# Sums over the keys by GpSimd in place of products with ones, in a decoder layer on one Trainium2 core

## The chip, the core and the metric

The kernel runs on one core of a Trainium2 chip. The core has a matrix engine (TensorE, PE in the profile, with PEld for its weight loads), a vector engine (VectorE, DVE), an engine for activation functions (ScalarE, ACT), a general engine (GpSimd, POOL) and an engine that only issues DMA transfers (SyncE, SP). Each works through its own queue in order and waits on semaphores for the others. TensorE writes to PSUM, a small memory of banks; the other engines read from there. The metric is the device time of one execution in microseconds, as the median of several runs.

## The reference

One decoder layer with a sequence of 512 tokens and a width of 1024, in float32. Two attentions run side by side on one projection of the normed input, and are merged behind gates:

```python
u = rms_norm(x, norm_mix_g[i])
proj = u @ w_in[i]
q_sb, k_sb, v_sb, q_dl, k_dl, v_dl, gate_sb, gate_dl = jnp.split(proj, SPLITS, axis=-1)
o_sb = stick_breaking_attention(heads_sb(q_sb), heads_sb(k_sb), heads_sb(v_sb))
o_dl = dilated_mixture_attention(heads_dl(q_dl), heads_dl(k_dl), heads_dl(v_dl)).astype(x.dtype)
merged = jax.nn.sigmoid(gate_sb) * (o_sb @ w_sb_up[i]) + jax.nn.sigmoid(gate_dl) * (o_dl @ w_dil_up[i])
x = x + merged @ w_out[i]
u2 = rms_norm(x, norm_ffn_g[i])
g_ff, up_ff = jnp.split(u2 @ w_ffn_in[i], 2, axis=-1)
x = x + (jax.nn.silu(g_ff) * up_ff) @ w_ffn_out[i]
```

Both attentions need a sum over keys. Stick-breaking (8 heads of 64) weighs key k for a query by exp(log sigmoid(z) + the sum of log sigmoid(-z) over the keys after k and before the query):

```python
log_keep = jnp.where(causal, jax.nn.log_sigmoid(-z), 0.0)
log_after = lax.cumsum(log_keep, axis=3, reverse=True) - log_keep
a = jnp.where(causal, jnp.exp(jax.nn.log_sigmoid(z) + log_after), 0.0)
```

The dilated attention (three groups of 4 heads, with window and dilation of their own and a bias by distance) is a softmax over the keys of all three groups; its denominator is a sum of exponentials over keys:

```python
p = jnp.exp(scores - m[..., None])
l = p.sum(-1)
...
den = (wts * jnp.stack(ls)).sum(0)
out = num / den[..., None]
```

## The kernel before

Activations lie with features on the 128 partitions and the 512 tokens in the free dimension. A weight chunk is 128 x 1024 numbers. Each number is split in two, a rounded high part and a low part (`hi`, `lo`), and `mm3` makes each product of three matmuls (lines 158 to 160): high by high, low by high, high by low. `weights(i, ahead=2)` keeps the split of chunks two ahead of the products: SyncE issues the load (line 111), ScalarE rounds (`whi`, line 143), VectorE takes the difference (`wlo`, line 144). `product` calls `tick()` after every three matmuls. The attentions are Python generators that are resumed at these ticks, so that their matmuls are issued between those of the projections; a `yield n` waits n ticks, and `can_take` waits until one of three pairs of PSUM banks is free (`take`, `give`). A planner that simulates the engines' time then fixes each engine's queue, by priorities and readiness. For the instructions on TensorE in the feed-forward part the order is written by hand.

*The beginning.* The first two weight chunks and the eight slices of x (tiles `x`, two slices each) are loaded in parts, one beside the other, on SyncE's queue; the norms' weights (`gt`, 128x24) by GpSimd's DMA queue (line 173). `norm_split` (lines 177 and 178) multiplies a slice of x by the norm's weight and splits it into `xh` and `xl`. The row factors of the norm are applied later, to the products. The first two products (`first`, query and key of pair 0) begin as the parts land. Behind the last split of x (`last_split`) ScalarE squares the four tiles of x (line 226), which VectorE adds up to `acc1`; the row sums over it (line 264) come on TensorE some ticks into the product for the values (`pvvs`), the first that uses the third weight chunk.

*Stick-breaking.* `sb_pair` handles two heads, four times. Scores are made with keys on the partitions in three parts: x holds query blocks 1 to 3 against key block 1 and query block 3 against key block 3 (128 x 2 x 512 in all), y key block 2 (128 x 2 x 256), z key block 0. `breaks` makes t = softplus of the scores from three activations and line 431, and splits it (lines 163 and 164). `weigh` adds the sums over later keys within the block by a product with a triangle of minus ones (line 439), and takes the exponential. What lies between blocks is a factor exp(-sum of t over all keys of a later block): `side` (line 446) multiplies t with ones on TensorE, so that each of the 64 partitions of a head holds the sum, the tile `b` takes these sums (parts x and y), and line 476 makes their exponentials `f` in one instruction on 128x768. `side` with values makes the weighted values, in `b` (part y) and `a`, and lines 486 to 492 put the blocks together with `f`.

*Dilated.* `dil_pair` handles two heads of each group, twice. Four score tiles `p` get the bias (line 519). The maximum over the groups is taken on VectorE, and over the partitions by GpSimd, `partition_all_reduce` (line 528), which leaves the result in every partition. After exponentials (lines 532 to 537) the groups are added to `mb` (lines 538 to 540). The numerator is `pn` (line 550). The denominator `dl` is a product of `mb` with ones (line 555), in a bank pair of its own; line 558 takes its reciprocal.

After the projections of the gates come the up-projections (`up`, whose second part reads the dilated output `ohd`), the output projection (`po`), and the feed-forward part with weights in seven forms (`pf`, `pg`) and the way down (`pd`). The residual is loaded by GpSimd's DMA queue (line 645).

Of the kernel before, what the change touches and what calls it, by code (L numbers as in the profile page):

```python
# [10 lines left out]
F32 = mybir.dt.float32  # L11
# [32 lines left out]
def trunk_kernel(ctx, tc, xT, gains, w_in, w_up, w_o, w_f, w_d, bias, out):  # L44
# [20 lines left out]
    def bank(tag, name):  # L65
# [4 lines left out]
        return pair(name)[:, 0, :]  # L70


    warm = cp.tile([P, P], BF16)
# [42 lines left out]
    def split_chunk(i):  # L116
# [24 lines left out]
        if kind in ("S23", "S1"):  # L141
            hi, lo = (t.rearrange("p (a n) -> p a n", a=2) for t in (hi, lo))
        A.copy(hi, r)  # L143
        V.tensor_tensor(out=lo, in0=r, in1=hi.bitcast(F32), op=ALU.subtract)  # L144
# [25 lines left out]
    fpool = [None]  # L170
    gt = cp.tile([P, 24], F32)
    g32 = cp.tile([P, KD], F32)
    nc.gpsimd.dma_start(out=gt, in_=gains)

# [38 lines left out]
    for k in range(KD):  # L213
# [4 lines left out]
        lo = xp.tile([P, S], F32R, tag=f"xl{k}", name=f"xl{k}")  # L218
        last_split = norm_split(k, xw[k // 2][:, k % 2, :], 0, hi, lo)
        if k % 2 == 0:  # L220
            split_to(parts[1][0][:, cs], parts[1][1][:, cs], raws[1][:, cs])
        xh.append(hi)
        xl.append(lo)
    with tc.high_priority():
        for x in xw:
            i = A.activation(x, x, AF.Square)
            tc.add_manual_dep(i.ins, last_split.ins.name, NOSYNC, reason="issue order")
        V.tensor_tensor(out=xw[0], in0=xw[0], in1=xw[1], op=ALU.add)
        V.tensor_tensor(out=xw[2], in0=xw[2], in1=xw[3], op=ALU.add)
        V.tensor_tensor(out=xw[0], in0=xw[0], in1=xw[2], op=ALU.add)  # L230
        V.tensor_tensor(out=acc1, in0=xw[0][:, 0, :], in1=xw[0][:, 1, :], op=ALU.add)
# [180 lines left out]
    def sb_pair(n, q, k, v, hb, done):  # L412
# [11 lines left out]
        def breaks(name, ps, w):  # L424
# [7 lines left out]
            split_to(hi, lo, t)  # L432
            return ps, t, hi, lo, lambda: new(f"e{n}{name}")


        def weigh(ps, t, hi, lo, new):
            for m in (hi, lo):
# [6 lines left out]
        def side(o, lhs, rhs, first):  # L444
            for h in range(2):
                T.matmul(o[hs[h]], lhs(h), rhs[:, h, :], start=first, stop=False, skip_group_check=True)

        yield can_take
        bx = breaks("x", scores("x", [(1, 0), (3, 384)]), S)
# [17 lines left out]
        val = lambda a: lambda h: v()[:, a, (hb + h) * 64:(hb + h + 1) * 64]  # L467
        one = lambda h: ones[:, :64]
        yield lambda: v() is not None
        yield can_take  # L470
        pb = take(f"b{n}")
        side(pb[:, 1, 0:384], one, bx[1][:, :, 0:384], True)
        side(pb[:, 1, 384:512], one, bx[1][:, :, 384:512], False)
        side(pb[:, 0, 256:512], one, by[1], True)
        f = wide(f"f{n}").rearrange("p a b -> p (a b)")[:, 256:1024]
        A.activation(f, pb.rearrange("p a b -> p (a b)")[:, 256:1024], AF.Exp, scale=-1.0)
        side(pb[:, 0, 0:256], val(2), ey, False)
        done.append(n)
# [28 lines left out]
    def dil_pair(n, q, k, v):  # L507
# [31 lines left out]
        V.tensor_tensor(out=by_block(mb), in0=by_block(t0), in1=by_token(m), op=ALU.add)  # L539
        V.tensor_tensor(out=mb[:, :, P:], in0=mb[:, :, P:], in1=t3[:, :, P:], op=ALU.add)  # L540
        yield 36
        yield lambda: v() is not None
        yield can_take
        pn = take(f"n{n}")
        for g in (1, 2, 0, 3):
            o = pn[:, int(g in (1, 2)), :]
            for c in range(g // 3, 4):
                for h in range(2):
                    cl = (2 * n + h) * 64
                    T.matmul(o[hs[h], cb[c]], v()[g % 3][:, c - g // 3, cl:cl + 64], tl[g][hs_all, h, cb[c]],  # L550
                             start=g < 2 and c == 0, stop=g > 1 and c == 3, skip_group_check=True)
        yield can_take
        pl = take(f"dl{n}")[:, 0, :]
        for h in range(2):
            T.matmul(pl[hs[h]], ones[:, :64], mb[:, h, :], start=True, stop=True)
        rl, nb = small(f"rl{n}"), small(f"nb{n}")
        A.copy(nb, pn[:, 1, :])
        V.reciprocal(rl, pl)
        nt = small(f"nt{n}")
        one = lambda t: t.unsqueeze(1)  # L560
        V.tensor_tensor(out=by_block(one(nt)), in0=by_block(one(pn[:, 0, :])), in1=by_token(one(nb)), op=ALU.add)
        V.tensor_tensor(out=rl, in0=nt, in1=rl, op=ALU.mult)
        give(6)
        give(6)
# [435 lines left out]
```

## Time and profile before

| | |
|---|---|
| median of the runs | 766.88 us (765.97, 766.88, 768.06) |
| the profiled execution's own time | 768.07 us |
| its span | 766.4 us |
| mean granted clock of TensorE | 0.995 |

The profile is of one execution. A row of a view in order of time gives start and duration in us, engine, line, operation, output <- input, shapes, and a count where neighbours are merged; the bracket says how long the engine had been idle and what ended it. A row of a tile's view gives minimum, median and maximum duration in ns, first and last start in us, and the forms. A row of stretches gives the length and for each engine its busy time with the number of instructions; its last row the sums. Matmuls overlap, and their ends are modelled: the distance between starts tells what one costs. Spans on POOL are rough.

### The profile page before, as it was taken

Reading aid. Unit: us, or ns where it says so; the run is one execution under the profiler, and the core shown is the slowest. Engines: PE = TensorE matmul, PEld = TensorE weight load, DVE = VectorE, ACT = ScalarE, POOL = GpSimd, SP = SyncE. Lnnn points to the kernel's source line nnn. Section 1 sums busy time; section 2 is a strip of 40 time slices with the busy share of each in tenths; the row PEclk is TensorE's granted clock in tenths of the full one; section 3 lists DMA queues with packets and bytes.
Section 4 is the critical chain, followed back from the end, with each engine's and each line's share of the span. In section 5 each row is a group of like instructions: output and inputs, shape, how many; then the busy total and the mean of one; then the engine's idle time right before and its main releaser. Section 6 shows DMA issues by size and latency. Waiting matters only on the chain. (4 is left out here: it accounts for less than half of the span.)

```text
span 766.4 us, 11025 instructions
## 1 busy us (share of the span) xinstructions
PE 753.4 (98%) x4498; PEld 646.6 (84%) x4498; DVE 511.6 (67%) x685; ACT 358.6 (47%) x509; POOL 29.0 (4%) x38
## 2 busy tenths in 40 slices
PE   8999999999999999999999999999999999999996
PEld 5877767798887878888788999999999999999985
DVE  6454646344677775358698989877788777776643
ACT  7273727462233352333455666544445454444453
POOL 1000000000101100000000100000000000000032
PEclk9999999999999999999999999999999999999998
DMA  7312121123224223233432223323333323332113
GB/s 247 137 56 83 56 83 56 56 69 124 83 83 159 88 84 103 62 91 129 145 103 79 75 89 103 103 79 122 98 106 114 103 82 113 100 105 77 56 55 111
DMA packets 24947, 74.13 MB, mean 97 GB/s; under 512 B 2736, under 2 KB 5824, under 8 KB 24768
## 3 DMA queue, kind: packets, MB, share of 16 engines
q1 hardware_dynamic: 23664, 69.87, 28.3%
q0 software_dynamic: 816, 3.16, 1.3%
q8 instruction: 35, 0.57, 0.3%
q10 hardware_dynamic: 416, 0.39, 0.2%
q14 instruction: 16, 0.13, 0.1%
HBM read 71.32 MB, written 2.10 MB: 96 GB/s over the span
## 5 line engine op out<-in xcount | busy, mean ns | idle before, releaser
L143 ACT CAST whi<-raw 128x1024 fp32r<-128x1024 f32 (+2 forms) x113 | 108.5, 962 | 160.8 <-issue 49.2
L144 DVE TENSOR_TENSOR wlo<-raw,whi 128x1024 fp32r<-128x1024 f32 (+2 forms) x113 | 125.9, 1115 | 34.4 <-ACT whi L143 33.6
L756 PE MATMUL pf<-fh,whi 128*128 128x256 f32 x348 | 98.8, 284 | 0.4 <-ACT q L763 0.3
L758 PE MATMUL pf<-fh,wlo 128*128 128x256 f32 x348 | 98.5, 283 | 0.0
L757 PE MATMUL pf<-fl,whi 128*128 128x256 f32 x348 | 98.5, 283 | 0.0
L756 PE MATMUL pg<-fh,whi 128*128 128x256 f32 x264 | 75.1, 285 | 0.6 <-ACT q L763 0.6
L757 PE MATMUL pg<-fl,whi 128*128 128x256 f32 x264 | 74.7, 283 | 0.0
L758 PE MATMUL pg<-fh,wlo 128*128 128x256 f32 x264 | 74.7, 283 | 0.0
L756 PEld LDWEIGHTS pf<-fh,whi 128*128 128x128 f32 x348 | 66.7, 192 | 1.5 <-ACT q L763 0.8
L757 PEld LDWEIGHTS pf<-fl,whi 128*128 128x128 f32 x348 | 66.7, 192 | 0.6
L758 PEld LDWEIGHTS pf<-fh,wlo 128*128 128x128 f32 x348 | 66.7, 192 | 0.3 <-DVE wlo L144 0.2
L144 DVE TENSOR_TENSOR wlo<-s,whi 128x1024 fp32r<-128x1024 f32 (+1 forms) x43 | 41.3, 960 | 15.9 <-ACT whi L143 15.7
L756 PEld LDWEIGHTS pg<-fh,whi 128*128 128x128 f32 x264 | 50.6, 192 | 1.1 <-ACT q L763 0.8
L143 ACT CAST whi<-s 128x1024 fp32r<-128x1024 f32 (+1 forms) x43 | 36.2, 841 | 32.6 <-PE pg L757 20.5
L757 PEld LDWEIGHTS pg<-fl,whi 128*128 128x128 f32 x264 | 50.7, 192 | 0.0
L758 PEld LDWEIGHTS pg<-fh,wlo 128*128 128x128 f32 x264 | 50.6, 192 | 0.0
L158 PE MATMUL pd<-hh,whi 128*128 128x512 f32 (+1 forms) x132 | 50.4, 382 | 0.0
L159 PE MATMUL pd<-hl,whi 128*128 128x512 f32 (+1 forms) x132 | 50.3, 381 | 0.0
L160 PE MATMUL pd<-hh,wlo 128*128 128x512 f32 (+1 forms) x132 | 50.1, 379 | 0.0
L143 ACT CAST whi<-rawu 128x1024 fp32r<-128x1024 f32 x22 | 23.1, 1051 | 28.4 <-PE pd L159 23.7
L853 DVE TENSOR_TENSOR res<-pd,res 128x512 f32<-128x512 f32 (+1 forms) x36 | 22.6, 629 | 19.5 <-PE pd L160 19.3
L160 PEld LDWEIGHTS pd<-hh,wlo 128*128 128x128 f32 x132 | 24.8, 188 | 4.8
(469 smaller groups left out, 1741.4 us busy)
## 6 DMA issues: line engine op xcount, KB each, us to landing
raw<-in_w_in_dram SPq DMA_DIRECT2D x44, 512.0 KB, 3.3
rawu<-in_w_ffn_in_dram SPq DMA_DIRECT2D x22, 512.0 KB, 3.3
raw<-in_w_ffn_in_dram SPq DMA_DIRECT2D x22, 512.0 KB, 3.4
raw<-in_w_ffn_out_dram SPq DMA_DIRECT2D x24, 384.0 KB, 3.2
raw<-in_w_out_dram SPq DMA_DIRECT2D x8, 512.0 KB, 3.3
raw<-in_w_up_dram SPq DMA_DIRECT2D x8, 384.0 KB, 3.0
x<-in_xT_dram SPq DMA_DIRECT2D x8, 256.0 KB, 4.6
res<-in_xT_dram POOLq DMA_DIRECT2D x8, 256.0 KB, 3.6
```

Source lines behind the costliest of these rows:

```text
L143: A.copy(hi, r)
L144: V.tensor_tensor(out=lo, in0=r, in1=hi.bitcast(F32), op=ALU.subtract)
L158: T.matmul(ps, shi, mhi, start=first, stop=False)
L159: T.matmul(ps, shi, mlo, start=False, stop=False)
L160: T.matmul(ps, slo, mhi, start=False, stop=last)
L756: T.matmul(ps, hi[:, cs], xhi, start=first and k == 0, stop=False, skip_group_check=True)
L757: T.matmul(ps, hi[:, cs], xlo, start=False, stop=False, skip_group_check=True)
L758: T.matmul(ps, lo[:, cs], xhi, start=False, stop=last and k == 3, skip_group_check=True)
L853: V.tensor_tensor(out=x, in0=ps, in1=x, op=ALU.add)
```

## The change

The sums over keys move from TensorE to GpSimd. In `breaks`, for parts x and y, a `partition_all_reduce` with addition writes the sum of t over the partitions to a new tile `sums[name]`, of the same shape as t. The products with ones in `side` are gone, and `f` is made from these sums, by four exponentials on 64 partitions each (for each head, part x with 512 columns and part y with 256). `b` holds only the weighted values of part y, whose first product now clears the bank. In `dil_pair` a second `partition_all_reduce` puts the sum of `mb` into `m` right behind line 540; two copies on ScalarE, one for each head's 64 partitions, bring it into `rl`, and the reciprocal is taken there. The bank pair `dl` is taken no more.

At the beginning the load of the norms' weights becomes the first instruction of the program, on ScalarE's DMA queue. `weights(0)` is called behind the loop over the slices of x, so that the third weight chunk is split there, and the four squares are ordered behind that chunk's rounding on ScalarE in place of behind the last split of x.

```diff
+    gt = cp.tile([P, 24], F32)
+    nc.scalar.dma_start(out=gt, in_=gains)
...
-        A.copy(hi, r)
+        state["last"] = A.copy(hi, r)
         V.tensor_tensor(out=lo, in0=r, in1=hi.bitcast(F32), op=ALU.subtract)
...
-    gt = cp.tile([P, 24], F32)
     g32 = cp.tile([P, KD], F32)
-    nc.gpsimd.dma_start(out=gt, in_=gains)
...
-        last_split = norm_split(k, xw[k // 2][:, k % 2, :], 0, hi, lo)
+        norm_split(k, xw[k // 2][:, k % 2, :], 0, hi, lo)
...
     with tc.high_priority():
+        weights(0)
         for x in xw:
             i = A.activation(x, x, AF.Square)
-            tc.add_manual_dep(i.ins, last_split.ins.name, NOSYNC, reason="issue order")
+            tc.add_manual_dep(i.ins, state["last"].ins.name, NOSYNC, reason="issue order")
...
             split_to(hi, lo, t)
-            return ps, t, hi, lo, lambda: new(f"e{n}{name}")
+            if name != "z":
+
+                sums[name] = new(f"s{n}{name}")
+                G.partition_all_reduce(sums[name].rearrange("p h q -> p (h q)"), t.rearrange("p h q -> p (h q)"), P, bass_isa.ReduceOp.add)
+            return ps, hi, lo, lambda: new(f"e{n}{name}")
...
         pb = take(f"b{n}")
-        side(pb[:, 1, 0:384], one, bx[1][:, :, 0:384], True)
-        side(pb[:, 1, 384:512], one, bx[1][:, :, 384:512], False)
-        side(pb[:, 0, 256:512], one, by[1], True)
         f = wide(f"f{n}").rearrange("p a b -> p (a b)")[:, 256:1024]
-        A.activation(f, pb.rearrange("p a b -> p (a b)")[:, 256:1024], AF.Exp, scale=-1.0)
-        side(pb[:, 0, 0:256], val(2), ey, False)
+        for h in range(2):
+            A.activation(f[hs[h], 256:768], sums["x"][hs[h], h, :], AF.Exp, scale=-1.0)
+            A.activation(f[hs[h], 0:256], sums["y"][hs[h], h, :], AF.Exp, scale=-1.0)
+        side(pb[:, 0, 0:256], val(2), ey, True)
...
+        G.partition_all_reduce(flat(m), flat(mb), P, bass_isa.ReduceOp.add)
         yield 36
...
-        yield can_take
-        pl = take(f"dl{n}")[:, 0, :]
+        rl, nb = small(f"rl{n}"), small(f"nb{n}")
         for h in range(2):
-            T.matmul(pl[hs[h]], ones[:, :64], mb[:, h, :], start=True, stop=True)
-        rl, nb = small(f"rl{n}"), small(f"nb{n}")
+            A.copy(rl[hs[h]], m[hs[h], h, :])
         A.copy(nb, pn[:, 1, :])
-        V.reciprocal(rl, pl)
+        V.reciprocal(rl, rl)
...
-        give(6)
         give(6)
```

More of the change, by code (lines that the diff above doesn't have):

```diff
@@ L432, in breaks, with weigh @@
             split_to(hi, lo, t)
[L433 to L436 removed]
+            if name != "z":
+                sums[name] = new(f"s{n}{name}")
+                G.partition_all_reduce(sums[name].rearrange("p h q -> p (h q)"), t.rearrange("p h q -> p (h q)"), P, bass_isa.ReduceOp.add)
+            return ps, hi, lo, lambda: new(f"e{n}{name}")
+        def weigh(ps, hi, lo, new):
             for m in (hi, lo):
@@ L446, in side @@
                 T.matmul(o[hs[h]], lhs(h), rhs[:, h, :], start=first, stop=False, skip_group_check=True)
+        sums = {}
         yield can_take
@@ L467, in sb_pair @@
         val = lambda a: lambda h: v()[:, a, (hb + h) * 64:(hb + h + 1) * 64]
-        one = lambda h: ones[:, :64]
         yield lambda: v() is not None
```

## The prediction

> **What bounds the kernel now.** I read the page's busy shares first, then the busy time in stretches of the attention stage, then TensorE's instructions in order of time around every product that the change takes out.
>
> ```profile
> span 766.4 us, 11025 instructions
> PE 753.4 (98%) x4498; PEld 646.6 (84%) x4498; DVE 511.6 (67%) x685; ACT 358.6 (47%) x509; POOL 29.0 (4%) x38
> ```
>
> ```profile
> sum 245.00, PE 245.00 PEld 189.91 DVE 141.35 ACT 115.41 POOL 11.58; mean PE 30.62 PEld 23.74 DVE 17.67 ACT 14.43 POOL 1.45
> ```
>
> The second fence is the sum of eight stretches that cover 41 to 286 us, where both attentions run: PE 245.00 of 245.00 us, VectorE 58%, ScalarE 47%, GpSimd 5%. So TensorE has no gap there, and the other engines have room. A busy PE by the modelled ends need not be at its peak, so I price the removed products by starts in the stream and not by their busy time. What comes after 286 us is unchanged by the diff and starts earlier by whatever TensorE saves.
>
> **The products with ones, stick-breaking.** TensorE around them in pair 0, in order of time (start, duration):
>
> ```profile
> 68.01 0.39 PE L160 MATMUL pjsq<-xh,wlo 128*128 128x512 f32 x1
> 68.33 1.08 PE L446 MATMUL b<-t0x,ones 128*64 128x384 f32 x8
> 69.24 0.60 PE L446 MATMUL b<-t0y,ones 128*64 128x256 f32 x4
> 69.77 0.50 PE L158 MATMUL pjsk<-xh,whi 128*128 128x512 f32 x1
> 70.11 0.39 PE L159 MATMUL pjsk<-xl,whi 128*128 128x512 f32 x1
> ```
>
> In a stretch of projections alone, TensorE's stream shows 26 steps between these two starts:
>
> ```profile
> 311.70 0.39 PE L159 MATMUL pjgs<-xl,whi 128*128 128x512 f32 x1
> ...
> 317.59 0.39 PE L158 MATMUL pjgs<-xh,whi 128*128 128x512 f32 x1
> ```
>
> That is 5.89 / 26 = 0.227 us for a step. Without the twelve, the start shown at 70.11 would come two such steps after 68.01, at 68.46. They cost 70.11 - 68.46 = 1.65 us, the two changes of matmul form included. Each of the four pairs has the same twelve. 4 x 1.65 = 6.6 us. The product with V that shared their bank keeps its own place and its own changes of form.
>
> **The products with ones, dilated.** The same view around pair 0's:
>
> ```profile
> 229.40 0.40 PE L160 MATMUL pjdk<-xh,wlo 128*128 128x512 f32 x1
> 229.73 1.08 PE L555 MATMUL dl<-mb,ones 128*64 128x512 f32 x4
> ...
> 231.07 0.39 PE L159 MATMUL pjgs<-xl,whi 128*128 128x512 f32 x1
> ```
>
> 231.07 - 229.40 - 2 x 0.227 = 1.22 us, twice: 2.4 us. TensorE loses 6.6 + 2.4 = **9.0 us** of work, all of it in the stretch without a gap.
>
> **What GpSimd takes on.** The kernel already runs one such reduction (a maximum, 128x1024) in each dilated pair. First GpSimd, then what VectorE did beside it and after it:
>
> ```profile
> 203.26 3.25 POOL L528 PARTITION_ALL_REDUCE mb<-m  x1 [26.89 <-DVE m L526]
> ...
> 257.21 3.22 POOL L528 PARTITION_ALL_REDUCE mb<-m  x1 [24.77 <-DVE m L526]
> ```
>
> ```profile
> 204.70 1.54 DVE L144 TENSOR_TENSOR wlo<-raw,whi 128x1024 fp32r<-128x1024 f32 x1 [0.17 <-ACT whi L143]
> ...
> 210.24 2.00 DVE L532 TENSOR_TENSOR p<-p,mb 128x1024 f32<-128x1024 f32 x1
> ```
>
> ```profile
> 258.81 1.37 DVE L144 TENSOR_TENSOR wlo<-raw,whi 128x1024 fp32r<-128x1024 f32 x1 [0.21 <-ACT whi L143]
> ```
>
> The recorded span is 3.2 us, and such spans are rough. The consumer L532 starts 6.98 us after the reduction does and waits for nothing, so 7.0 us is a firm upper end. An addition over 128x1024 I put at 3.2 (the same instruction on the same shape), at most 7.0; the 128x512 one at 1.6 by half the columns, also at most 7.0. GpSimd gets 4 x (3.2 + 1.6) + 2 x 3.2 = 26 us, at most 4 x 14 + 14 = 70, and it is idle in nearly all of the 245. Its queue holds little else there: the load of the biases, which waits for the last pair's products anyway, and the loads of the residual, needed only for the output projection after the up-projection.
>
> Is a sum there in time? Pair 0, VectorE, then the line of the first consumer's row in the same view:
>
> ```profile
> 51.43 1.23 DVE L431 SCALAR_TENSOR_TENSOR t0x<-z0x,t0x 128x1024 f32<-128x1024 f32 x1 [2.60 <-ACT t0x L430]
> 53.77 1.23 DVE L164 TENSOR_TENSOR l0x<-t0x,h0x 128x1024 fp32r<-128x1024 f32 x1 [0.52 <-ACT h0x L163]
> 75.02 0.56 DVE L487 TENSOR_TENSOR o<-a,f 128x384 f32<-128x384 f32 x1 [4.51 <-ACT o L486]
> ```
>
> t0x is final at 52.66 and f is needed at 75.02: 22.4 us, less the exponentials. Two reductions of 4.8 us, or even 14, fit. Their cost on the path is 0; the cover is gone only above about 20 us for the two.
>
> ScalarE's exponential on 128x768 becomes four on half the partitions:
>
> ```profile
> 49.81 0.64 ACT L429 ACTIVATE t0y<-t0y 128x512 f32<-128x512 f32 x1
> ...
> 69.89 0.82 ACT L476 ACTIVATE f<-b 128x768 f32<-128x768 f32 x1 [0.64 <-PE b L446]
> ```
>
> Four are at most 4 x 0.64 = 2.56, so at most 1.74 more in each pair, 7.0 in all, plus in each dilated pair two copies of at most 0.64 on the way to the reciprocal, 2.6 in all: under 10 us on an engine that is idle 130 of the 245. No half-partition instruction stands in this trace; below, nothing is gained that matters. I cost it at 0, under the idle time of ScalarE.
>
> In the dilated pair the sum now takes a reduction and two copies (at most 7.0 + 1.3) where TensorE took 1.1:
>
> ```profile
> 278.00 0.94 DVE L540 TENSOR_TENSOR mb<-mb,p 128x768 f32<-128x768 f32 x1
> ```
>
> ```profile
> L158 PE MATMUL up<-ohd,whi x16: 389/389/389, 331.2 to 360.4; 128*128 128x512 f32 x16
> ```
>
> For the later pair that is 278.94 + 8.3 = 287.2, then a reciprocal and two short operations, done before 300. The up-projection wants it at 331. Cost 0. One bank is taken less, so later score products can only come sooner.
>
> **The beginning.** Two moves. The gains go from GpSimd's DMA queue to the head of ScalarE's. What ScalarE, VectorE and TensorE waited for:
>
> ```profile
> 4.63 0.72 ACT L177 ACTIVATE xh<-x,gt 128x512 fp32r<-128x512 f32 x1 [0.86 <-DMA gt<-in_gains_dram]
> 6.44 0.72 ACT L177 ACTIVATE xh<-x,gt 128x512 fp32r<-128x512 f32 x1 [0.79 <-DMA x<-in_xT_dram]
> 7.20 0.75 DVE L178 SCALAR_TENSOR_TENSOR xl<-x,gt,xh 128x512 fp32r<-128x512 f32 x1 [0.73 <-ACT xh L177]
> 8.00 0.19 PEld L159 LDWEIGHTS first<-xl,whi 128*128 128x128 f32 x1 [0.57 <-DVE xl L178]
> ```
>
> The wait for the gains goes, at most 0.86 us. But the second slice of x lands at 6.44 whatever the gains do, and it sets the weight load and matmul at 8.00, from which TensorE runs without a stop that the gains could lift. What is late next is that slice, so I take 0; a small load ahead of it may shift it by some tenths either way, say 0.5.
>
> The second move: the third chunk of weights is split before the four squares. TensorE, ScalarE, and the row of the loads L111 that are issued between 9.2 and 19.4:
>
> ```profile
> 17.22 0.39 PE L160 MATMUL first<-xh,wlo 128*128 128x512 f32 x1
> 18.18 0.97 PE L158 MATMUL pvvs<-whi,xh 128*128 128x512 f32 x3 [0.57 <-ACT whi L143]
> 19.44 0.50 PE L159 MATMUL pvvs<-wlo,xh 128*128 128x512 f32 x1 [0.29 <-DVE wlo L144]
> ...
> 22.06 0.39 PE L159 MATMUL pvvs<-wlo,xh 128*128 128x512 f32 x1
> ```
>
> ```profile
> 14.26 2.94 ACT L226 ACTIVATE x<-x 128x1024 f32<-128x1024 f32 x3
> 17.10 1.03 ACT L143 CAST whi<-raw 128x1024 fp32r<-128x1024 f32 x1
> 18.04 1.06 ACT L226 ACTIVATE x<-x 128x1024 f32<-128x1024 f32 x1
> ```
>
> ```profile
> DMA to landing us min/median/max: 3.1/4.2/5.6
> ```
>
> Fourteen matmuls start from 18.18 up to 22.06. At 0.227 they would run from 17.45 to 20.62; they end 22.06 - 20.62 = 1.4 us late, which is what the three squares ahead of the cast cost. The chunk's load is issued at 9.20 and lands by 9.20 + 5.6 = 14.8 at the latest. Cast 1.03 and difference 1.23 after it give 17.1, before 17.45. I take **1.4 us**; the other end is 0, if the load comes later. The squares then end near 20 instead of 19.1. Their sum is used by the row sums only at 29 us, ten steps behind, so it stays hidden; and the casts of the next two chunks come about 0.2 us later, with their products 5 us off.
>
> **The sum.** 9.0 + 1.4 = 10.4 us. The profiled execution took 768.07 with a span of 766.4; less 10.4 that is 757.7. The median of the runs shown is 766.88, 1.2 below it, so I forecast 766.88 - 10.4 = **756.5 us**. Its own range: nothing gained at the beginning and the runs' scatter (765.97 to 768.06, about 1 us) give 758.9; 0.5 more and the scatter on the other side, 754.9.
>
> **The rivals.** *A wait on ScalarE.* The engine works in order. If the exponentials f stand in its queue ahead of z's logarithms and cast, and the reductions take 7 + 7 us, they wait until 52.66 + 14 = 66.7; behind them stand z's cast and the next weights, and the running sum z, at 65.9 on TensorE, waits. For 66.7 + 2.6 + 1.0 for the cast that is 4.4 us a pair, 17.6 in all: 774. At half of that excess the time is 765, and at the 3.2 us of the record, nothing. Against it: the kernel's order left seven us between the reduction and L532, so its planner counts such a reduction as long. Middle value 761.
>
> *Nothing is won.* If the split weights, not TensorE, set the pace of these products, the gap only moves: 766. VectorE at 58% and the missing waits on TensorE speak against it.
>
> *Slower: VectorE held by GpSimd.* The reductions read the same memory as VectorE's differences of two operands, and one falls right ahead of l0x. If VectorE were locked out for as long as both reductions of a pair run (L together), l0x would end L + 1.23 after 52.66, and TensorE wants it at 59.03. The last pair has the least room:
>
> ```profile
> 151.82 1.23 DVE L431 SCALAR_TENSOR_TENSOR t3x<-z3x,t3x 128x1024 f32<-128x1024 f32 x1 [3.55 <-ACT t3x L430]
> ```
>
> ```profile
> L439 PE MATMUL z0x<-l0x,tri x2: 390/394/398, 59.0 to 59.3; 128*128 128x512 f32 x2
> ...
> L439 PE MATMUL z3x<-l3x,tri x2: 392/394/395, 157.7 to 157.9; 128*128 128x512 f32 x2
> ```
>
> Leads 6.4 and 4.6 us; take 6 for the mean. It costs 4 x (L + 1.2 - 6), which eats the 10.4 from L = 7.4 on. At L = 14 it is 37 us: 793. For it: the difference at 204.70 took 1.54 us beside the reduction, against 1.23 where GpSimd was idle. Against it: it took 0.3 more, not 2, and that of 258.81 ended at 260.18 while the reduction was recorded to 260.43. The Trainium skill, SBUF — State Buffer, section Who interferes with whom, has the rule that would make this rival true: an operation of VectorE with two inputs in SBUF and a GpSimd operation that reads SBUF exclude each other, and the loser blocks for the whole instruction. These two rows show a delay of a few tenths and no block, so I keep the chance low.
>
> *Slower: an addition over partitions is far dearer than the maximum.* It decides from about 20 us for a pair, as above; were each of them 25 us, f would come some 30 us late in each of four pairs and the time be near 860. No row here shows an addition. The same instruction with a maximum, at most 7.0 us, speaks against it. The Trainium skill, GPSIMD Engine Reference, section Cross-partition — where GPSIMD wins, gives 247.7 us for a reduction along the partitions of 128x2048; half, an estimate of 124 us for 128x1024 from that page, would put the kernel above 1000 us. The trace's 3.2 to 7.0 us disagrees for the maximum.
>
> **How the numbers follow.** Forecast 0.77; wait on ScalarE 0.10; nothing won 0.06; VectorE held 0.05; dear addition 0.02. The range takes the forecast's own, 754.9 to 758.9, and the cheaper part of ScalarE's wait, to 760.8. A measurement of this kernel tells 0.3% (2.3 us) from no change; by that the first two cases count as faster, 0.87, the third as the same, 0.06, the last two as slower, 0.07.
>
> **What would show it.** Right: no gap between projection matmuls where 68.33 and 229.73 stood; reductions of 3 and under 2 us beside a PE that stays full; pvvs directly behind first at about 17.45. Wrong: idle time of PE in front of L439 with VectorE or ScalarE as its releaser, f's exponentials waiting for GpSimd, differences l0x of clearly more than 1.23 us, or a first pvvs that waits for its raw load.

## The result and the profile after

The changed kernel takes 759.37 us (median of six runs, 758.90 to 760.94); the kernel before 767.80 (six runs, 765.97 to 769.62). The ratio over all these runs is 0.9895, 95% interval 0.9877 to 0.9912: about 8.1 us or 1.05% less (the two medians differ by 8.4). The forecast was 756.5 with a range up to 760.8. The direction was right; the saving is some two us short of the 10.4 forecast, and the stages show that less of it came from where the prediction put it than the total says.

The profiled executions took 768.07 before and 759.12 after. The changed kernel's page, span and busy time, and then the sum of eight stretches that cover 41 to 277 us, both attentions again:

```profile
span 757.4 us, 10944 instructions
PE 745.9 (98%) x4442; PEld 644.9 (85%) x4442; DVE 533.0 (70%) x685; ACT 365.0 (48%) x525; POOL 78.1 (10%) x47
```

```profile
sum 236.00, PE 235.01 PEld 185.72 DVE 159.27 ACT 118.42 POOL 59.60; mean PE 29.38 PEld 23.22 DVE 19.91 ACT 14.80 POOL 7.45
```

TensorE has 7.5 us less busy time, GpSimd 49 us more where 26 were expected, and VectorE is busy 21.4 us longer with as many instructions as before: some of its instructions must have become longer. And TensorE, full before in this stage, now has a hole of 0.99 us. The reductions on GpSimd, in order of time (start, duration), pairs 0 and 3 of stick-breaking and the second dilated pair:

```profile
51.29 6.13 POOL L437 PARTITION_ALL_REDUCE s0x<-t0x  x1 [17.76 <-DVE t0x L432]
57.34 3.32 POOL L437 PARTITION_ALL_REDUCE s0y<-t0y  x1
...
146.95 6.12 POOL L437 PARTITION_ALL_REDUCE s3x<-t3x  x1 [19.99 <-DVE t3x L432]
152.97 3.31 POOL L437 PARTITION_ALL_REDUCE s3y<-t3y  x1
...
249.90 3.22 POOL L532 PARTITION_ALL_REDUCE mb<-m  x1 [23.12 <-DVE m L530]
271.80 6.11 POOL L545 PARTITION_ALL_REDUCE m<-mb  x1 [18.68 <-DVE mb L544]
```

L532 is the maximum that was there before, and L545 the addition on the same 128x1024: 3.2 us against 6.1. VectorE beside them:

```profile
51.07 0.68 DVE L432 SCALAR_TENSOR_TENSOR t0y<-z0y,t0y 128x512 f32<-128x512 f32 x1
52.27 4.64 DVE L166 TENSOR_TENSOR l0x<-t0x,h0x 128x1024 fp32r<-128x1024 f32 x1 [0.52 <-ACT h0x L165]
56.83 0.68 DVE L166 TENSOR_TENSOR l0y<-t0y,h0y 128x512 fp32r<-128x512 f32 x1
57.43 0.68 DVE L356 SCALAR_TENSOR_TENSOR sq<-pjsq,rb 128x512 f32<-128x512 f32 x1
58.03 2.72 DVE L146 TENSOR_TENSOR wlo<-raw,whi 128x1024 fp32r<-128x1024 f32 x1
```

The subtraction l0x, 1.23 us before, is recorded with 4.64. It starts 0.98 us after the reduction s0x does and ends at 56.91. With 1.23 us of work, it could go on at 55.68, so it was held until 4.4 us after the reduction's start, and the last 1.7 us of the reduction, as far as a span on POOL can be trusted, hold nobody. wlo in the last row, by the same reading, is let go at 59.52, 2.2 us after s0y started. It reads other tiles than the reduction does, so a shared tile isn't the reason. L356 takes one operand from PSUM and runs at its usual 0.68; t0y, which reads PSUM too, likewise. (PSUM is read here by VectorE and ScalarE only; the reductions of GpSimd read and write tiles in SBUF, the large on-chip memory.) The pattern repeats in every pair (l1x 3.91, l2x 4.69, l3x 4.67). TensorE feels it once. The list of its waits has this line, and the row in order of time stands behind it:

```profile
PE z3x L444 <- DVE l3x L166: 1.0, 1, 1.0
```

```profile
152.62 0.73 PE L444 MATMUL z3x<-l3x,tri 128*128 128x512 f32 x2 [0.99 <-DVE l3x L166]
```

Where the time went by stages is read from the first start of some products, before and after (the views of the tiles z0x, z3x, up and ss: minimum, median and maximum duration in ns, then first and last start):

```profile
L417 PE MATMUL z0x<-sq,sk x8: 269/377/587, 45.8 to 46.7; 64*128 64x384 f32 x4, 64*128 64x128 f32 x4
L417 PE MATMUL z3x<-sq,sk x8: 269/377/587, 146.7 to 147.6; 64*128 64x384 f32 x4, 64*128 64x128 f32 x4
L158 PE MATMUL up<-ohs,whi x32: 389/389/389, 328.5 to 359.1; 128*128 128x512 f32 x32
L264 PE MATMUL ss<-ones,acc x8: 168/250/250, 423.6 to 424.3; 128*128 128x1 f32 x8
```

```profile
L418 PE MATMUL z0x<-sq,sk x8: 269/377/587, 44.3 to 45.2; 64*128 64x384 f32 x4, 64*128 64x128 f32 x4
L418 PE MATMUL z3x<-sq,sk x8: 269/377/587, 140.3 to 141.2; 64*128 64x384 f32 x4, 64*128 64x128 f32 x4
L160 PE MATMUL up<-ohs,whi x32: 389/389/389, 319.9 to 350.5; 128*128 128x512 f32 x32
L265 PE MATMUL ss<-ones,acc x8: 168/250/250, 414.7 to 415.4; 128*128 128x1 f32 x8
```

| stage | before | after | saved |
|---|---|---|---|
| start to z0x | 45.8 | 44.3 | 1.5 |
| z0x to z3x (three pairs) | 100.9 | 96.0 | 4.9 |
| z3x to up (fourth pair, dilated pairs, gates) | 181.8 | 179.6 | 2.2 |
| up to ss | 95.1 | 94.8 | 0.3 |
| ss to the end of the span | 342.8 | 342.7 | 0.1 |

Three pairs save 4.9, 1.63 each: that is the 1.65 of the forecast. Between z3x and up, where 1.65 + 2.4 = 4.1 were to come, it is 2.2. The 1.5 at the start look like the forecast's 1.4, but they are something else. The stretch 30 to 35 us, before and then after (columns: length, then busy time of PE, PEld, DVE, ACT and POOL with instructions, granted clock, DMA share, GB/s):

```profile
30.00:35.00 5.00, 5.00 (x17) 4.37 (x17) 0.66 (x2) 1.04 (x1) 1.67 (x1) 0.66 0.00 0
```

```profile
30.00:35.00 5.00, 5.00 (x23) 4.40 (x24) 1.39 (x2) 1.06 (x1) 1.66 (x1) 1.00 0.10 41
```

In the profiled execution of before the granted clock fell to 0.66 there. TensorE in order of time, behind the row sums:

```profile
29.09 2.81 PE L264 MATMUL rows<-ones,acc 128*128 128x1 f32 x16
31.77 0.77 PE L158 MATMUL pvvs<-whi,xh 128*128 128x512 f32 x1
32.34 0.63 PE L159 MATMUL pvvs<-wlo,xh 128*128 128x512 f32 x1
...
34.81 0.40 PE L159 MATMUL pvvs<-wlo,xh 128*128 128x512 f32 x1
```

Eight steps take 34.81 - 31.77 = 3.04 us; at 0.227 they take 1.82. So 1.2 of the 1.5 is the clock of this one execution, and the beginning itself gave 0.3. A kernel of the experiments below, the one with the reductions unused, bears this out: it has the old beginning and no fall of the clock in its profiled execution, and its z0x starts at 44.5. What the change did there is also not what was forecast. SyncE's queue after, and the row of before for the same load:

```profile
1.71 0.42 SPq L207 DMA_DIRECT2D raw<-in_w_in_dram  x1
2.18 0.43 SPq L113 DMA_DIRECT2D raw<-in_w_in_dram  x1
```

```profile
9.20 0.43 SPq L111 DMA_DIRECT2D raw<-in_w_in_dram  x1
```

`weights(0)` stands inside `high_priority`, and the third chunk's load is issued from within it: it went to 2.18, ahead of seven slices of x, where the forecast left it at 9.20. The products with that chunk then fill TensorE while x arrives later:

```profile
8.46 1.48 PE L160 MATMUL pvvs<-whi,xh 128*128 128x512 f32 x3
```

### The profile page after: what moved, and what is told of

Read it like the earlier page. It is cut to its first block, busy times and chain, and to the rows that moved or that the text cites. A ratio compares the mean times of both kernels' runs of the same rounds, so it can differ in the third digit from the quotient of the medians.

```text
span 757.4 us, 10944 instructions
## 1 busy us (share of the span) xinstructions
PE 745.9 (98%) x4442; PEld 644.9 (85%) x4442; DVE 533.0 (70%) x685; ACT 365.0 (48%) x525; POOL 78.1 (10%) x47
## 4 chain that ended last, share of the span: by engine, by line
PE 92%; DVE 3%; DMA 2%; ACT 1%; issue 1%; POOLq 0%; SPq 0%; POOL 0%; DVEq 0%; ACTq 0%
PE pf L758 5%; PE pd L160 5%; PE pd L161 5%; PE pd L162 5%; PE pf L759 5%; PE pf L760 5%; PE pg L758 4%; PE pg L760 4%; PE pg L759 4%; PE pjgs L160 2%; PE pjgd L160 2%; PE pjgs L162 2%; PE pjgd L162 2%; PE pjgs L161 2%; PE pjgd L161 2%; PE pjdk L160 2%
## 5 line engine op out<-in xcount | busy, mean ns | idle before, releaser
L145 ACT CAST whi<-raw 128x1024 fp32r<-128x1024 f32 (+2 forms) x113 | 108.5, 962 | 156.7 <-PE pg L759 32.7
L146 DVE TENSOR_TENSOR wlo<-raw,whi 128x1024 fp32r<-128x1024 f32 (+2 forms) x113 | 133.1, 1179 | 43.2 <-ACT whi L145 42.4
L861 POOL TENSOR_TENSOR inv<-inv,sq 128x256 f32<-128x256 f32 (+1 forms) x10 | 9.6, 961 | 318.1 <-ACT sq L860 315.9
```

What stands on the lines that cost most here:

```text
L145: state["last"] = A.copy(hi, r)
L861: G.tensor_tensor(out=rows["inv"][:, cs], in0=rows["inv"][:, cs], in1=sq[:, cs], op=ALU.add)
```

## The experiments

The theory: the removed products are worth what they were priced at; VectorE's subtractions are shut out by the reductions, which costs one wait of 1 us; the beginning is worth little. Rivals: the beginning did its work, the hold of VectorE costs nothing, or the time is eaten elsewhere.

**The beginning alone.** The kernel before with the first hunks of the change only (the load of the gains, `weights(0)` ahead of the squares).

```diff
+    nc.scalar.dma_start(out=gt, in_=gains)
...
-    nc.gpsimd.dma_start(out=gt, in_=gains)
...
+        weights(0)
```

> The kernel before with the change at the beginning alone: gains loaded first on ScalarE's queue, third weight chunk split ahead of the squares, products with ones left on TensorE. Theory (the two parts add up): the first score product of pair 0, at 45.84 us before and 44.34 us after the change, starts near 44.3, and the time is 1.5 us below that of before (0.998). Rival (what the beginning showed was a chance of the clock, which ran slow for some microseconds at another place in each of the two profiles): no measurable difference, within 0.5 us.

Ratio 1.0003 (0.9991 to 1.0015), twelve runs. No gain can be measured, though the row sums start at 28.25 instead of 29.09 and z0x at 45.4 instead of 45.8 in the profiled execution, which has the same fall of the clock to 0.66 behind the row sums.

**The sums alone.** The changed kernel with the old beginning.

> The changed kernel with the beginning of before: the sums alone. Theory: products taken out 8.7 us, less 1.25 us for the wait of the last pair's running sum on VectorE's difference and 0.4 us for score products in the dilated part: 7 us below before (ratio 0.991). Rival (the sums won all of the 9.0 us forecast and the beginning nothing): 9 us, 0.988.

Ratio 0.992 (0.9903 to 0.9938), 761.41 us, with the wait of 1.0 us at z3x. So most of the gain, 0.8 of 1.05%, is in the sums. That the two parts give 0.0 and 0.8% by themselves and 1.05% together is within the intervals; the clock explains part of it, see below.

**Without the stick-breaking reductions.** The exponentials read t itself, so the kernel leaves out these sums over keys.

```diff
-                sums[name] = new(f"s{n}{name}")
-                G.partition_all_reduce(sums[name].rearrange("p h q -> p (h q)"), t.rearrange("p h q -> p (h q)"), P, bass_isa.ReduceOp.add)
+                sums[name] = t
```

> The changed kernel without the eight reductions of stick-breaking: the exponentials f read t itself, so the factors between blocks are left out; the reductions in the dilated part stay. Theory (a reduction holds VectorE): the differences l0x to l3x fall from 4.6 us to 1.2 us each, TensorE's wait in front of the last pair's running sum (1.0 us) goes, and the kernel is 1.2 us faster than the changed one, 0.988 of before. Rival (the difference was slow for another reason, or TensorE's wait is of the planner's order): l3x stays above 3 us or the wait remains, and the time that of the changed kernel, 0.9895.

Ratio 0.9875 (0.9857 to 0.9893), 757.72 us. VectorE in order of time at the fourth pair:

```profile
147.73 1.23 DVE L166 TENSOR_TENSOR l3x<-t3x,h3x 128x1024 fp32r<-128x1024 f32 x1 [0.24 <-ACT h3x L165]
```

The subtractions are back at 1.23, the wait at z3x is gone, and z3x to up takes 178.4 us against 179.6: between these two starts the hold costs 1.2 us. The intervals of the two kernels overlap, so the time alone wouldn't carry this; the two traces do.

**Maximum in place of addition.** Both sums over keys are left out in this way.

```diff
-                G.partition_all_reduce(sums[name].rearrange("p h q -> p (h q)"), t.rearrange("p h q -> p (h q)"), P, bass_isa.ReduceOp.add)
+                G.partition_all_reduce(sums[name].rearrange("p h q -> p (h q)"), t.rearrange("p h q -> p (h q)"), P, bass_isa.ReduceOp.max)
...
-        G.partition_all_reduce(flat(m), flat(mb), P, bass_isa.ReduceOp.add)
+        G.partition_all_reduce(flat(m), flat(mb), P, bass_isa.ReduceOp.max)
```

> The changed kernel with a maximum in place of the addition in the ten new reductions, so the sums over keys are left out. Theory (the addition itself is the slow one, and VectorE is held for a part of the recorded span): 128x1024 is recorded at 3.2 us as for the old maximum, l0x ends some 1.8 us after the reduction starts plus its own 1.2 us, which makes it about 2 us long in place of 4.6, and TensorE's wait for l3x goes: 0.988 of before. Rival (a maximum does not hold VectorE, as the forecast read its two rows): l0x 1.2 to 1.5 us. Second rival (the place and not the operation is what makes it slow): 6.1 us for the maximum too, no change against the changed kernel.

Ratio 0.988 (0.9862 to 0.9898), 758.4 us. GpSimd and VectorE, pair 0:

```profile
50.45 3.25 POOL L437 PARTITION_ALL_REDUCE s0x<-t0x  x1 [17.76 <-DVE t0x L432]
53.61 2.06 POOL L437 PARTITION_ALL_REDUCE s0y<-t0y  x1
```

```profile
51.43 2.00 DVE L166 TENSOR_TENSOR l0x<-t0x,h0x 128x1024 fp32r<-128x1024 f32 x1 [0.52 <-ACT h0x L165]
```

The maximum is the 3.2 us of the forecast; the addition is 1.9 times as long. Here l0x ends at 53.43 and could go on at 52.20, 1.75 us after the reduction's start, and TensorE no longer waits at z3x. So the maximum holds VectorE as the addition does, for a shorter time.

**Each reduction in two, one for each head.**

```diff
-                G.partition_all_reduce(sums[name].rearrange("p h q -> p (h q)"), t.rearrange("p h q -> p (h q)"), P, bass_isa.ReduceOp.add)
+                for h in range(2):
+                    G.partition_all_reduce(sums[name][:, h, :], t[:, h, :], P, bass_isa.ReduceOp.add)
```

> The changed kernel with each of the eight stick-breaking reductions in two, one for each head (512 and 256 columns). Theory (VectorE is held by the reduction that is running, and gets in between two): l3x waits for one half, 2.2 us of its 3.3, and ends some 2.2 us earlier than in the changed kernel; TensorE's wait of 1.0 us in front of the last pair's running sum goes, and the kernel is 1.2 us faster than the changed one, 0.988 of before. Rival (VectorE stays held through reductions that follow each other): l3x is as long as before, 4.6 us, the wait stays, 0.9895.

Ratio 0.9887 (0.9875 to 0.99), 758.72 us. Two halves take 6.45 us together, and VectorE gets in between them:

```profile
147.29 2.38 DVE L166 TENSOR_TENSOR l3x<-t3x,h3x 128x1024 fp32r<-128x1024 f32 x1 [0.24 <-ACT h3x L165]
149.59 2.76 DVE L166 TENSOR_TENSOR l3y<-t3y,h3y 128x512 fp32r<-128x512 f32 x1
```

l3x costs 2.38 instead of 4.67, but the second half then holds l3y, and TensorE waits 0.6 us for that one at z3y instead of 1.0 at z3x. Of the kernels that compute everything it has the lowest median, 0.65 us under the change, and the intervals don't tell the two apart.

**Each reduction twice.**

```diff
-                G.partition_all_reduce(sums[name].rearrange("p h q -> p (h q)"), t.rearrange("p h q -> p (h q)"), P, bass_isa.ReduceOp.add)
+                for _ in range(2):
+                    G.partition_all_reduce(sums[name].rearrange("p h q -> p (h q)"), t.rearrange("p h q -> p (h q)"), P, bass_isa.ReduceOp.add)
```

> The changed kernel with each of the eight stick-breaking reductions run twice, the second writing the same. Theory (VectorE held): in pair 0 l0y waits for the second reduction of part x, to about 62.5, where TensorE wants it at 61.2, and z's difference comes some 5 us late behind a next weight chunk that is held twice; waits of VectorE show on TensorE in every pair, and the time is 8 to 20 us above the changed kernel's, 767 to 780. Rival (GpSimd's work is hidden as long as f is in time, which needs about 20 us a pair): not above 761.

Ratio 0.9954 (0.9941 to 0.9968), 763.29 us. It fell between the two theories. l0y, which the first theory had wait, takes its usual 0.68: GpSimd runs s0x, s0y and then both again, so the repeats hold later subtractions. But the kind of the waits is the theory's, all for subtractions that VectorE made late (and one of 0.5 us more at z2z):

```profile
PE z0z L445 <- DVE l0z L166: 1.2, 1, 1.2
PE z1z L445 <- DVE l1z L166: 1.2, 1, 1.2
...
PE z3x L445 <- DVE l3x L166: 0.6, 1, 0.6
PE pvvd L161 <- DVE wlo L146: 0.6, 1, 0.6
```

The waits of this kind are 4.1 us together, against 1.0 in the changed kernel. The repeat of s0x and the subtraction that it holds show one thing more:

```profile
60.47 6.19 POOL L438 PARTITION_ALL_REDUCE s0x<-t0x  x1
62.90 3.26 DVE L166 TENSOR_TENSOR l0z<-t0z,h0z 128x1024 fp32r<-128x1024 f32 x1 [1.12 <-ACT h0z L165]
```

l0z starts 2.43 us into the addition, and taking 1.23 from its end, 66.16, it was let go 4.46 us after the addition's start. l0x in the changed kernel started 0.98 into it and was let go after 4.39. The point of release doesn't depend on when the subtraction comes, so the subtraction stands still until then and isn't merely slowed.

**The third chunk's load put back behind the slices of x**, in the changed kernel, and then together with the halves.

```diff
+    dma_chunk(2)
+    state["dma"] = 3
     with tc.high_priority():
         weights(0)
```

> The changed kernel with the third chunk's load behind the slices of x on SyncE's queue, as before the change; the split of the chunk still stands ahead of the squares. Theory (the third split ahead of the squares is worth 1.4 us, which the load ahead of x takes back in the first 10 us): first runs as in the kernel before from 8.0 us on, pvvs starts directly behind it near 17.5, and the time is 1 us below the changed kernel's in traces of one clock. Rival (the beginning is worth nothing either way): no difference above the runs' scatter, and the first score product of pair 0 not before 44.3.

Ratio 0.9934 (0.9922 to 0.9947), 761.8 us: slower than the change, at equal clock too (five runs at 0.995 have a mean span of 760.6 us, two of the change 759.0), and the theory fell on the time. The beginning itself came as forecast, with pvvs at 17.25 directly behind `first` and no wait. But the planner's order came out another way, with projections ahead of the first scores (z0x at 47.6 instead of 44.3) and a split of weights ahead of l0x. The trace also has the fall of the clock (0.79 and 0.87 in the stretches 30 to 35 and 35 to 40 us). VectorE in order of time, and TensorE's wait:

```profile
55.42 4.64 DVE L146 TENSOR_TENSOR wlo<-raw,whi 128x1024 fp32r<-128x1024 f32 x1
59.98 1.21 DVE L166 TENSOR_TENSOR l0x<-t0x,h0x 128x1024 fp32r<-128x1024 f32 x1
61.12 2.72 DVE L166 TENSOR_TENSOR l0y<-t0y,h0y 128x512 fp32r<-128x512 f32 x1
```

```profile
PE z0y L446 <- DVE l0y L166: 1.6, 1, 1.6
```

Now the first reduction holds the weights and the second holds l0y, which was late already; the wait of 1.0 us at z3x is there as well.

> Both of the edits of this job on the changed kernel: the third chunk's load behind the slices of x, and the stick-breaking reductions one head at a time. Theory (both losses are real and independent): 1.2 + 1.0 us below the changed kernel, 0.9865 of before, near 757.3. Rival (one of the two is no loss): 0.988 to 0.9895.

Ratio 0.9913 (0.9898 to 0.9928), 760.38 us, with waits of 0.6 at z3y and 0.3 at z0y. Halving the hold took 1.4 us off the late load's time, though the intervals overlap a little; the waits say why.

**The beginning alone, with the late load**, in the kernel before.

> The kernel before with the beginning of the change but the third chunk's load behind the slices of x, products with ones left on TensorE. Theory (the split ahead of the squares is worth the 1.4 us of the stall at 18 us, and the early load takes part of it back): pvvs starts right behind first at about 17.3, no wait there, and the time is 1.4 us below before, 0.998, if both fall on the same clock. Rival (nothing of the beginning reaches the end): 1.000.

Ratio 1.0001 (0.9987 to 1.0015), twelve runs. In its trace TensorE goes from `first` into the third chunk at once, as the forecast had it:

```profile
17.37 0.84 PE L160 MATMUL pvvs<-whi,xh 128*128 128x512 f32 x3
```

Its wait of 0.6 us for the third chunk's rounding is gone, and nothing of that can be measured at the end. In the trace some of it is there: z1x starts at 77.7, and at 78.4 in the kernel with the old beginning and the reductions unused, both without a fall of the clock. So the forecast's mechanism is there, worth about 0.7 us in the traces at that point, and its 1.4 us are not.

**The dilated sums back on TensorE**, the rest of the change kept.

```diff
-        G.partition_all_reduce(flat(m), flat(mb), P, bass_isa.ReduceOp.add)
...
-            A.copy(rl[hs[h]], m[hs[h], h, :])
+        pl = take(f"dl{n}")[:, 0, :]
...
+            T.matmul(pl[hs[h]], ones[:, :64], mb[:, h, :], start=True, stop=True)
```

> The changed kernel with the dilated sums back on TensorE, as before the change. Theory (dilated products 2.4 us, of which 0.4 is lost again in score products): 2.0 to 2.4 us above the changed kernel, 0.992 of before. Rival (VectorE, held by the reductions there too, gave the gain back): no difference to the changed kernel, 0.9895.

Ratio 0.9908 (0.9892 to 0.9925), 760.52 us: 1.15 above the change, between the two expectations, and the intervals overlap. The trace is plainer. The first product of the up-projection:

```profile
L160 PE MATMUL up<-ohs,whi x32: 389/389/389, 322.4 to 353.0; 128*128 128x512 f32 x32
```

With z3x at 140.4 that makes 182.0 us from z3x to up against 179.6: the 2.4 us of the forecast. From up to ss it is 94.0 us against 94.8. Between 350 and 425 us the change has two waits, 1.0 us together, of the feed-forward's first products `pf` for the tile `q` from ScalarE (L765), and this kernel has none there: about 0.8 of the 2.4 is given back to waits on ScalarE. That TensorE comes earlier isn't reason enough: the sums alone reach up at 322.2, as late as this kernel, and have 1.3 us of such waits. All kernels here with the dilated sums on GpSimd have between 0.7 and 1.5 us of them in this stretch, and none of the others has any; why stays open.

**The reductions unused, in the kernel before.**

```diff
+            if name != "z":
+                s = new(f"s{n}{name}")
+                G.partition_all_reduce(s.rearrange("p h q -> p (h q)"), t.rearrange("p h q -> p (h q)"), P, bass_isa.ReduceOp.add)
```

> The kernel before with the eight stick-breaking reductions added, into tiles that nothing reads; products with ones stay on TensorE. What GpSimd's sums cost by themselves. Theory (VectorE held for about two thirds of each): l0x to l3x near 4.6 us, a wait of TensorE in front of a running sum in the last pair, 1.2 us above before, 1.0016. Rival (a reduction costs nothing unless its result is waited for): no wait on VectorE's differences, 1.000.

Ratio 1.0019 (1.0008 to 1.0029), 769.2 us, twelve runs; the theory held. GpSimd's sums by themselves cost 1.5 us, and the trace shows where: z3x to up takes 183.0 us against 181.8 of before, with

```profile
PE z3x L442 <- DVE l3x L164: 1.0, 1, 1.0
```

which the kernel before doesn't have. Together with the kernel without reductions, which shows the same 1.2 us with the opposite sign, this puts the price of the hold between z3x and up at 1.2 us.

**Each reduction behind the subtraction of its own split.**

```diff
-            split_to(hi, lo, t)
+            late = split_to(hi, lo, t)
...
-                G.partition_all_reduce(sums[name].rearrange("p h q -> p (h q)"), t.rearrange("p h q -> p (h q)"), P, bass_isa.ReduceOp.add)
+                red = G.partition_all_reduce(sums[name].rearrange("p h q -> p (h q)"), t.rearrange("p h q -> p (h q)"), P, bass_isa.ReduceOp.add)
+                tc.add_manual_dep(red.ins, late.ins.name, SYNC, reason="behind the split")
```

> The changed kernel, with each stick-breaking reduction on GpSimd made to wait for the subtraction of its own split on VectorE, and nothing left out. Theory (the whole loss of the fourth pair is that the reduction starts ahead of the subtraction and shuts it out): the subtractions of the x parts take 1.2 us again instead of 3.9 to 4.7, what is held instead is a split of weights or a later part's subtraction with more time to spare, TensorE's 1.0 us wait at z3x goes, and the time is 1.25 us under the changed kernel's: about 758.1 us, a ratio of 0.988 to the kernel before. Rival (the hold only moves: VectorE is shut out for as long in all, and the next subtraction in the queue is needed just as soon): another wait of 0.5 us or more stands on TensorE at a part y or z, and the ratio is 0.9895 or more.

Ratio 0.9889 (0.9873 to 0.9906), 759.24 us: neither the one nor the other. VectorE, fourth pair and the split behind it:

```profile
148.44 1.23 DVE L167 TENSOR_TENSOR l3x<-t3x,h3x 128x1024 fp32r<-128x1024 f32 x1 [0.25 <-ACT h3x L166]
...
152.59 3.15 DVE L147 TENSOR_TENSOR wlo<-raw,whi 128x1024 fp32r<-128x1024 f32 x1 [2.33 <-ACT whi L146]
```

The x parts are back at 1.23 and the wait at z3x is gone; the hold moved to the splits of weights, and a wait of 0.2 us for one stands at `pvvd`. But the planner ordered the products another way: the first pair takes 0.4 us longer (z0x to z1x 32.7 us against 32.3), and z3x to up takes 179.3, only 0.3 less than with the wait. Removing the wait is shown; that it makes the kernel faster is not. The order of the two instructions shows who is held: s3x now starts at 149.86, inside l3y (149.58, 0.68 us as usual), and its record is 6.38 us instead of 6.12. VectorE, which came first, kept its pace, and GpSimd took 0.26 us longer.

**The clock, over all runs.** Each run lists its span and its mean granted clock. The mean spans in us, with the number of runs, at the clocks where both the kernel before and another of the four have runs (the other clocks are left out):

| granted clock | before | beginning alone | sums alone | the change |
|---|---|---|---|---|
| 0.998 | 764.7 (9) | none | 757.8 (1) | 757.4 (3) |
| 0.997 | 765.3 (17) | 765.4 (4) | none | 757.8 (1) |
| 0.995 | 766.8 (19) | 765.8 (5) | 760.0 (5) | 759.0 (2) |

From 0.998 to 0.995 the kernel before loses 2.1 us, a quarter of the whole gain. (The runs of before are those of all comparisons.) At equal clock the change is 7.3 to 7.9 us under before, the sums alone 6.8 to 6.9, and the beginning is worth between 0 and 1. Differences of 1 us and less are at the limit of this reading: the unused reductions, whose trace shows 1.2 us, come out at 0.0 us at 0.995 (4 runs) and at 1.7 us at 0.996 (5 runs, 767.9 against 766.2). Why a run gets the one clock or the other stays open: the fall behind the row sums stands in the profiled executions of before, the beginning alone, the sums alone and both late-load variants of the change, and in no other of these kernels, the late load without the sums among them.

## Why the prediction was right, and where it was not

**The removed products** (9.0 us) were sized right where they can be seen alone: 4.9 us over three pairs, 4.95 forecast, and 2.4 for the dilated sums by the kernel that puts them back. Pricing by starts in the stream and not by busy time was what made it so. The fourth pair and the dilated ones together show 2.2 of 4.1: 1.2 goes with the hold of l3x (1.0 of it the wait at z3x). Of the remaining 0.7, 0.4 is in the score products `d` of the first dilated pair: from start to start the 60 take 4.6 us against 4.1 before, because the planner cut them into groups of 22, 10, 18 and 10 where it had been 16, 16, 16 and 12. In the kernel whose reductions wait behind the subtractions the groups are the old ones, and they take 4.1 again. The last 0.3 stays open.

**"An addition over 128x1024 I put at 3.2 (the same instruction on the same shape)"** was mis-sized: it takes 6.1 us, and over 128x512 3.3, not 3.2 and 1.6. The upper bound of 7.0, from the consumer's start, held. Being in time wasn't hurt: s0y is done at 60.66, and f's exponentials start at 66.50 without a wait, 0.62 and 0.40 us, each twice: 2.05 us for the four, at most 2.56 forecast.

```profile
66.50 0.62 ACT L479 ACTIVATE f<-s0x 64x512 f32<-64x512 f32 x1
67.02 0.40 ACT L480 ACTIVATE f<-s0y 64x256 f32<-64x256 f32 x1
```

So the rival of ScalarE's wait didn't come, nor the dear addition. (The sum of that last rival was also off in itself: four times 30 us on 756.5 make 876, not 860.) The Trainium skill's figure of 247.7 us for 128x2048 (GPSIMD Engine Reference, section Cross-partition — where GPSIMD wins) is for `tensor_reduce`, another instruction; half of it, an estimate of 124 us for 128x1024 from that page, is twenty times the 6.1 us that the trace shows for `partition_all_reduce`.

**"These two rows show a delay of a few tenths and no block"** is the step that failed. The two rows of before did show the block, and the prediction misread them. The maximum started at 203.26, and wlo beside it started at 204.70 and took 1.54 us. Taking 1.23 from its end, 206.24, gives 205.01: it was let go 1.75 us after the reduction's start. The other pair gives 258.81 + 1.37 - 1.23 - 257.21 = 1.74. They had come 1.4 and 1.6 us into a hold of 1.75 and met only its tail; the same 1.75 came out with the maximum in the new place. A short delay is evidence against a lock only if the other instruction started at its beginning. And the recorded end of the reduction, 260.43, isn't the end of the hold, so a subtraction that ended before it proved nothing. The rule of the Trainium skill (SBUF — State Buffer, section Who interferes with whom) that two-operand work of VectorE in SBUF and a GpSimd instruction that reads SBUF exclude each other holds here, and so does its other half, that VectorE's work with one operand in SBUF is left alone. That the loser waits for the whole instruction, which the section says of VectorE's two-port modes, doesn't fit the record of these subtractions: 4.4 of 6.1 us, 1.75 of 3.2, by recorded spans of GpSimd that are rough.

The signs that the prediction named for this, idle time of PE in front of the running sums with VectorE as its releaser and differences of clearly more than 1.23, both came. So the rival's mechanism was real, its chance of 0.05 rested on the misreading, and its price was too high. It took the holds of both reductions as one: with the measured L = 4.4 + 2.2 = 6.6 its sum, 4 x (6.6 + 1.2 - 6), gives 7.2 us, where the runs show 1.2. VectorE gets in between the two, so only x's 4.4 counts. With the subtraction's own 1.2 that is 5.6 us, against leads of 6.4 and 4.6 us: the first pair is in time, and the fourth is 1.0 late.

**The beginning** (1.4 us) wasn't there. The load of a chunk that is asked for under high priority is moved on SyncE's queue too, and the forecast left it at 9.20. With it left there, TensorE did what was forecast, and the kernel was still no faster. The step that failed is that a stall removed at 18 us is won at the end. What can be said is 0 to 1 us at equal clock, and why not more stays open.

**The sum.** Of 10.4 us forecast, the trace gives 9.0, and 1.2 of that is the clock of the profiled execution of before; 7.8 are the kernel's. The differences: the hold in the fourth pair 1.2, the beginning 1.1, the other losses between z3x and up 0.7, and 0.4 to the good between up and the end. The baseline of three runs, 766.88, was also 0.9 under the six runs' median. So part of the hit is luck: 759.37 lies above the forecast's own 758.9 and is covered only by the piece of the range that was added for ScalarE's wait, which didn't come.

## What to carry to other kernels

A reduction moved to an idle engine isn't free when its instructions shut out those of a busy one: count the hold on every instruction that can meet it, and see which has the least lead. To judge a lock from an old trace, work out when the shorter instruction could go on and compare that with the start of the longer one; the delay alone depends on when it came. And where a few tenths of a per cent are at stake, compare several runs at each granted clock, and read a stage from two starts inside it, so that a fall of the clock elsewhere isn't credited to the change.

## What the runs showed of the hardware

Adding over 128 partitions is recorded on GpSimd with 1.9 times the maximum for 128x1024 (6.12 against 3.22 us) and with 3.3 to 3.8 us against 2.1 to 2.6 for 128x512, and two halves cost 6.45 us where one whole costs 6.12. The hold on VectorE's subtractions ends 4.4 us into an addition over 128x1024 whether they come 0.98 or 2.43 us into it, well before the recorded end, and an operation of VectorE that waits gets in between two reductions that follow each other directly. The 16 products of one column for the row sums are followed, in some executions, by some 3 us in which TensorE's steps take 0.43 us instead of 0.227; that alone is 1.2 us, as much as the hold in the fourth pair cost.
